# Second feed-forward: the down projection of the last eight tiles by seven products of blocks, with weight sums made by adding DMAs

## The chip, the core and the metric

The kernel runs on one core of a Trainium2 chip. The metric is the device time of one launch in microseconds (us). Executions of this kernel lie close together: three runs gave 1104.26 to 1104.41 us, median 1104.38 us. TensorE (PE) multiplies, VectorE (DVE), ScalarE (ACT) and GpSimd (POOL) work on elements, and SyncE (SP) issues almost all DMAs, in the order of its program.

## What is computed

One layer of a hybrid transformer: a half-step gated feed-forward, a token mixing with attention and a gated MLP, and a second half-step feed-forward. Everything is modulated by vectors made from `c` and `w_ada`. The parts that matter here:

```python
def swiglu(h, w1, w3, w2):
    return (jax.nn.silu(h @ w1) * (h @ w3)) @ w2

def ffn_sublayer(h_in, shift, scale, gate, norm_w, w1, w3, w2):
    h = modulate(rms_norm(h_in, norm_w), shift, scale)
    return h_in + 0.5 * gate * swiglu(h, w1, w3, w2)

mx = jnp.split((jax.nn.silu(c) @ w_ada + b_ada)[:, None, :], N_MOD, axis=-1)
x = ffn_sublayer(x, mx[0], mx[1], mx[2], norm1_w, ffn1_w1, ffn1_w3, ffn1_w2)
...
x = ffn_sublayer(x, mx[6], mx[7], mx[8], norm3_w, ffn2_w1, ffn2_w3, ffn2_w2)
```

`x` has 512 tokens of width 1024, `ctx` 256 tokens; the inner width of a feed-forward is 2816, that is 22 tiles of 128 (`NF`). All values are float32.

## The kernel before

**Three passes for a product.** A float32 operand is split into a rounded part and a remainder ("h" and "l": `st.operand`, `split`, one cast on ACT and one subtraction on DVE), and `mm3` (L173) multiplies h by h, h by l and l by h.

**Start (up to 49 us).** The first scale and shift vectors need 8 MB of `w_ada`, eight steps of two 512 KB rows. For each step k, `first_rows(k)` and `first_raw(k)` load a `scale` tile (1 MB) and a piece of the first up weights (`wfirst`, 256 KB). PE multiplies the rows (L338), ACT and DVE turn the result into one slice of the modulated input (`hfull`, `hh`, `hl`), and PE multiplies that slice with the first weights (L616). Two loads bring the context tokens (`x<-xT 128x8x128`). These loads are pinned to their order among themselves; what has no such pin and waits for nothing is put by the scheduler wherever a queue's model has room. The products of the context tokens follow (L601).

**Up projections by seven products.** From tile 4 on, both feed-forwards compute an up tile f (its two weight blocks by two halves of the width, against two halves of the tokens) in the class `Winograd` by seven block products in place of eight. One unit loads a 1 MB weight block (`st.block`, SP), and POOL makes four sums and differences of its 128x512 quarters in place (`s<-block`, `block<-block`, `block<-s,block`). Each of the seven operands is split by ACT and DVE, up to five ahead of PE (`Flow`, `OPS`; the second feed-forward gets four more, `MORE`). `unit` sends seven products of 12 matmuls through `product`, and small evacuations combine the four banks (`ev_u2z`, `ev_u3`, `ev_lo`, `ev_hi`) into the gated tile `gt[f]`.

**Down projections plainly.** When a chunk of up tiles is ready, `down_thirds` (first feed-forward) or `down_flow` (second) multiplies them with w2, 8 output tiles by n up tiles by 3 passes, and adds to x. The second one's chunks are `CHUNKS2 = [4, 4, 4, 4, 2, 4]`; the last is done by `down` after the loop, with one matmul over 512 columns for each pass and with output DMAs behind each evacuation (L412, L406).

**What sets the order.** The first feed-forward's instructions are placed by the scheduler under dependencies and a pin on parts of the start; in the second the order on PE, DVE, ACT and POOL is that of the program (`nc.ordered`). SP takes its DMAs in the order the scheduler gives, and a DMA that waits for a semaphore holds all DMAs behind it. The wait names DMAHW0 to DMAHW7 are eight semaphores used in turn, so at most eight DMAs of SP are under way.

Of the kernel before, what the change touches and what calls it, by code (L numbers as in the profile page):

```python
# [17 lines left out]
P = 128  # L18
# [12 lines left out]
STEPS_T = (0, 2, 4, 3, 3, 4, 4, 4)  # L31
CHUNKS2 = [4, 4, 4, 4, 2, 4]
NFIRST = 2
# [3 lines left out]
BLOCKS = 2  # L37
# [38 lines left out]
class Halves:  # L76
# [5 lines left out]
    def __getitem__(self, key):  # L82
        i = key[1].start // 512
        return self.tiles[i][:, key[1].start - 512 * i : key[1].stop - 512 * i]


# [95 lines left out]
def layer_kernel(ctx: ExitStack, tc: tile.TileContext, xT, wfirst, wst, wada, wuq, wkpe, cols, wrope, vnw, rope, out):  # L182
# [3 lines left out]

    const = ctx.enter_context(tc.tile_pool(name="const", bufs=1))
    raws = ctx.enter_context(tc.tile_pool(name="raws", bufs=RAWS))
    opp = ctx.enter_context(tc.tile_pool(name="ops", bufs=1))
# [634 lines left out]
    U_UP2 = U_IN + 22  # L824
    U_DN2 = U_UP2 + 44

# [12 lines left out]
    class Winograd:  # L839


        def __init__(self, pool, n, u0, blocks, g_tile, sl_bufs, s1_bufs, third=None, held=None):
            self.third, self.held = third, held
            self.sl_bufs, self.s1_bufs = sl_bufs, s1_bufs
            self.ready = (None,)
            self.pool, self.n, self.u0, self.blocks, self.g_tile = pool, n, u0, blocks, g_tile

        def tmp(self, name, n, bufs=1):
            return self.pool.tile([P, n], F32, tag=name, bufs=bufs, name=f"{name}_{nc.next_id()}")

        def prep(self, f, eng=None, early=False):
            r = st.block(wst, (self.u0 + 2 * f) // 2, self.third if f % 3 == 0 else None)
            q = [r[:, i * 512 : i * 512 + 512] for i in range(4)]
            s1 = self.tmp("s1", 512, self.s1_bufs)
            if f != self.held:
                (eng or nc.gpsimd).tensor_add(s1, q[2], q[3])
            if early:
                eng.tensor_sub(q[2], q[0], q[2])
            self.ready = f, q, s1, nc.gpsimd if early else eng or nc.gpsimd, early

        def wants(self, f):
            q, s1, eng = [], [], []

            def first():
# [6 lines left out]
                return a  # L871

            def block_sums():
                if not self.ready[4]:
                    eng[0].tensor_sub(q[2], q[0], q[2])
                eng[0].tensor_sub(q[0], s1[0], q[0])

# [8 lines left out]
            def third():  # L886
                a = st.operand(q[1])
                eng[0].tensor_sub(q[1], q[1], q[0])
                return a
# [4 lines left out]
        def plan(self, flow, f0, downs, late=False):  # L894
# [3 lines left out]
            flow.todo.append(w[0])  # L898
            for f in range(f0, NF):
                nxt = self.wants(f + 1) if f + 1 < NF else None  # L900
                nx = nxt[:1] if nxt else ()
                if f == self.late:
                    flow.todo.extend((w[3], w[4], w[2]) + nx + (w[1],) + w[5:])
                elif nxt is None:
                    flow.todo.extend((w[3], w[4], w[2], w[1]) + w[5:])
                else:
                    flow.todo.extend(w[1:5] + nx + w[5:])
# [4 lines left out]
        def product(self, bank, blk, first, pend, step=None, cut=False):  # L912
            flow = self.flow
            a = flow.take()
            if blk == "T3" and flow.size > OPS:
                flow.size -= 1
            flow.slot(step or (lambda: None))
            prod(bank, a, self.blocks[blk], self.n, first, cut)
            flow.spent = 1
            flow.pend = [pend] if pend else []  # L920

        def open(self, f, step, f0=None, splits=()):
# [11 lines left out]

            self.product(banks[0], "B11", True, evac(), step)
            return banks, p1

        def unit(self, f, hd, step):
# [7 lines left out]
            def ev_sl():  # L946
                nc.scalar.activation(sl, X, AF.Silu)
                yield

            def ev_u2():  # L950
                v.tensor_add(u2, Y, p1)
                yield

            def ev_u2z():
                v.tensor_add(u2, Y, p1)
                yield
                v.tensor_add(Z, Z, u2)

            def ev_u3():
                nc.scalar.copy(u3, W)  # L960
                v.tensor_add(u3, Z, u3)
                yield

            def ev_lo():
                v.tensor_add(W, W, u2)
                v.tensor_mul(W, W, sl)
# [3 lines left out]
            def ev_hi(seeded=False):  # L970
# [3 lines left out]
                nc.scalar.activation(Z, Z, AF.Silu)  # L974
                v.tensor_mul(Z, Z, u3)
                g_split(Z, gh[:, n:], gl[:, n:])
# [9 lines left out]
            nxt = None  # L986
            if f == self.late or f + 1 == NF:
                self.product(banks[1], "T2", True, ev_u2(), lambda: step(f, 0))
# [5 lines left out]
            else:  # L994
# [3 lines left out]
                self.product(banks[3], "T3", True, ev_u3())  # L998
            seeded = f != self.late and f + 1 < NF
            if f + 1 < NF and nxt is None:  # L1000
                nxt = self.open(f + 1, None)
            self.product(banks[3], "T4", False, ev_lo(), lambda: step(f, 3))
            self.product(banks[2], "B22", False, ev_hi(seeded), cut=n > 256 and f in DOWN1)
            return nxt

        def run(self, flow, f0, after, step=lambda f, i: None, opening=None, splits=()):
# [3 lines left out]
            for f in range(f0, NF):  # L1010
                hd = self.unit(f, hd, step)
                after(self.flow, f)
            flow.slot()
            other_banks()

    def evac_part(pt, dt, g, n):
# [13 lines left out]
    def after1(flow, f):  # L1030
        for ci in ends1(f):
            down_thirds(flow, starts1[ci], CHUNKS1[ci], lambda dt: ada_step(2))

    def ada_up(f, i):
# [3 lines left out]
        elif i < 2:  # L1038
            ada_step()

    t1ctx = ExitStack()
# [1102 lines left out]
    gt.clear()  # L2144
    f2.tile([P, 16], F32, bufs=1, name="pad_f2")

    def g2_tile(f):
        gt[f] = tuple(f2.tile([P, 512], F32R, tag=t, bufs=6, name=f"{t}_{nc.next_id()}") for t in ("gh", "gl"))
        return gt[f]
# [50 lines left out]
    def diffs(i, j, between):  # L2200
# [8 lines left out]
        for k, (hA1, hA2, hB1, hB2) in zip((i, j), q):  # L2209
            s = mod_s[2][0][:, k + 4 : k + 5]  # L2210
            nc.scalar.activation(T2[0][:, k, :], hB2, AF.Identity, bias=s)
            nc.vector.tensor_sub(hA2, hA2, hB2)
        between()
# [10 lines left out]
    def ends2(f):  # L2224
        return [ci for ci in range(len(CHUNKS2) - 1) if starts2[ci] + CHUNKS2[ci] == f]

# [44 lines left out]
    blocks = {"B11": B11, "B21": B21, "B22": B22, "T1": T1, "T2": T2, "T3": T3, "T4": T4}  # L2271
    wino = Winograd(f2, 256, U_UP2, blocks, g2_tile, 2, 2, f2, NPLAIN2 + 1)
    wino.prep(NPLAIN2, nc.vector)
# [23 lines left out]

    def ev3(pt, dt, g, gn):
        evac_lat(pt, dt, 2)
        nc.sync.dma_start(two(out[:, dt, :]), lat(x, dt))  # L2300

    def ev_half(pt, dt, g, gn):
        evac_x(pt, dt, seg_of(g // 256)[:1], 2)
        o = slice(g // 256 * 384, g // 256 * 384 + 256)
        nc.sync.dma_start(out[:, dt, g : g + 256], x[:, dt, o])

    def after2(flow, f):
# [3 lines left out]
    nc.ordered = "all"  # L2311
    st.more = f2ctx.enter_context(tc.tile_pool(name="ops2", bufs=1)), MORE
    wino.run(flow, NPLAIN2, after2, splits=splits)
    nc.ordered = False
    lastu = {}
    last2 = (starts2[-1], CHUNKS2[-1], U_DN2 + starts2[-1])
    down(*last2, [(0, 512)], ev3, range(NK - 1), lastu)
    down(*last2, [(0, 256), (256, 256)], ev_half, range(NK - 1, NK), lastu)
    f2ctx.close()
# [100 lines left out]
```

## Time and profile before

| | |
|---|---|
| median of three runs | 1104.38 us |
| profiled execution, its own time | 1104.5 us |
| span, from the first to the last instruction | 1102.5 us |
| PE busy, share of the span | 1097.5 us, 100% |
| DVE, ACT, POOL busy | 892.8, 536.5, 310.3 us |
| granted clock of PE | 1.00 |
| bytes from HBM, to HBM | 122.58 MB, 2.10 MB |

The difference of 2.0 us between the execution's own time and its span lies outside the instructions. A matmul's busy time is from its start to its modelled end and overlaps the next one's; what PE takes for a stretch of work is read from the chain of waits, which counts from start to start.

### The profile page before, as it was taken

How to read it: one execution, taken by the hardware profiler on the slowest of the kernel's cores; microseconds unless marked ns; L12 is line 12 of the kernel's file. 1: busy time of each engine (PE TensorE's matmuls, PEld its weight loads, DVE VectorE, ACT ScalarE, POOL GpSimd, SP SyncE). 2: the span in 40 equal slices, each digit the busy share in tenths (PEclk: the TensorE clock that was granted, in tenths of full speed). 3: DMA queues.
4: the chain of work that ended last, by engine and by line, in shares of the span. 5: the costliest groups of instructions: out<-in, count | busy, mean ns of one | idle time of the engine just before them, and what ended most of it. 6: DMA issues, size and time to landing. Idle time of an engine off the chain costs nothing.

```text
span 1102.5 us, 19621 instructions
## 1 busy us (share of the span) xinstructions
PE 1097.5 (100%) x7610; PEld 1052.5 (95%) x7610; DVE 892.8 (81%) x1594; ACT 536.5 (49%) x1115; POOL 310.3 (28%) x269
## 2 busy tenths in 40 slices
PE   9999999999999999999999999999999999999998
PEld 7899999999999999999998889999999989898997
DVE  5779998888878769866867899989988878787883
ACT  6545422431344214443765549986663535354450
POOL 0003303311344013400009317860014444352420
PEclk9999999999999999999999999999999999999999
DMA  9721354234334664412241310103222322424202
GB/s 354 279 60 47 120 172 139 100 137 148 106 124 151 233 201 164 149 54 93 97 132 61 102 50 21 39 21 102 91 94 89 123 78 93 137 78 132 99 21 77
DMA packets 35677, 125.95 MB, mean 114 GB/s; under 512 B 3712, under 2 KB 10624, under 8 KB 30976
## 3 DMA queue, kind: packets, MB, share of 16 engines
q1 hardware_dynamic: 35440, 124.63, 33.2%
q8 instruction: 60, 0.98, 0.4%
q14 instruction: 33, 0.27, 0.1%
q10 hardware_dynamic: 144, 0.06, 0.1%
HBM read 122.58 MB, written 2.10 MB: 113 GB/s over the span
## 4 chain that ended last, share of the span: by engine, by line
PE 96%; DMA 1%; DVE 1%; ACT 1%; POOL 0%; issue 0%; SPq 0%; ACTq 0%; POOLq 0%; DVEq 0%
PE mm L60 61%; PE one L60 20%; PE big L60 10%; PE big L616 1%; PE mm L601 1%; DMA scale<-wada 1%; PE mm L177 1%; PE mm L176 1%; PE mm L178 1%; PE mm L338 1%; DMA x<-xT 0%; PE big L608 0%; DVE sq L60 0%; POOL pe L60 0%; ACT hh L60 0%
## 5 line engine op out<-in xcount | busy, mean ns | idle before, releaser
L60 DVE TENSOR_TENSOR opl<-block,oph 128x512 fp32r<-128x512 f32 x216 | 195.4, 912 | 32.6 <-ACT oph L60 29.9
L60 POOL TENSOR_TENSOR block<-block 128x512 f32<-128x512 f32 x69 | 105.0, 1522 | 378.9 <-DVE opl L60 376.2
L60 ACT CAST oph<-block 128x512 fp32r<-128x512 f32 x216 | 132.3, 622 | 108.8 <-PE mm L60 85.5
L60 PE MATMUL mm<-gl,oph 128*128 128x256 f32 (+2 forms) x573 | 176.4, 308 | 0.0
L60 PE MATMUL mm<-gh,opl 128*128 128x256 f32 (+2 forms) x573 | 176.4, 308 | 0.0
L60 PE MATMUL mm<-gh,oph 128*128 128x256 f32 (+2 forms) x573 | 176.4, 308 | 0.0
L60 PEld LDWEIGHTS mm<-gh,oph 128*128 128x128 f32 x573 | 107.6, 188 | 5.5
L60 PEld LDWEIGHTS mm<-gh,opl 128*128 128x128 f32 x573 | 107.6, 188 | 5.4
L60 PEld LDWEIGHTS mm<-gl,oph 128*128 128x128 f32 x573 | 107.6, 188 | 5.4
L60 ACT CAST oph<-raw 128x512 fp32r<-128x512 f32 x127 | 76.0, 620 | 69.7 <-PE mm L60 44.4
L60 DVE SCALAR_TENSOR_TENSOR x<-mm,g,x 128x512 f32<-128x512 f32 (+2 forms) x136 | 78.7, 600 | 28.5 <-PE mm L60 27.9
L60 DVE TENSOR_TENSOR opl<-raw,oph 128x512 fp32r<-128x512 f32 x127 | 88.1, 710 | 15.3 <-ACT oph L60 14.0
L60 POOL TENSOR_TENSOR block<-s,block 128x512 f32<-128x512 f32 x35 | 48.3, 1379 | 123.8 <-DVE opl L60 122.3
L60 PE MATMUL mm<-hh,oph 128*128 128x384 f32 (+2 forms) x195 | 64.9, 333 | 0.0
L60 PE MATMUL mm<-hl,oph 128*128 128x384 f32 (+2 forms) x195 | 64.8, 333 | 0.0
L60 PE MATMUL mm<-hh,opl 128*128 128x384 f32 (+2 forms) x195 | 64.8, 333 | 0.0
L60 DVE SCALAR_TENSOR_TENSOR junk<-raw,cb 128x1024 bf16<-128x1024 f32 x48 | 62.1, 1308 | 0.2 <-DMA raw<-wada 0.2
L60 POOL TENSOR_TENSOR s<-block 128x512 f32<-128x512 f32 x34 | 53.7, 1579 | 11.4 <-DMA block<-wst 11.4
L60 DVE SCALAR_TENSOR_TENSOR raw<-raw,cb 128x1024 f32<-128x1024 f32 x32 | 42.1, 1322 | 8.3 <-DMA raw<-wada 8.2
L60 PE MATMUL one<-hl,oph 128*128 128x384 f32 x144 | 48.1, 334 | 0.0
L60 PE MATMUL one<-hh,oph 128*128 128x384 f32 x144 | 48.1, 334 | 0.0
L60 PE MATMUL one<-hh,opl 128*128 128x384 f32 x144 | 48.1, 334 | 0.0
(699 smaller groups left out, 3361.9 us busy)
## 6 DMA issues: line engine op xcount, KB each, us to landing
raw<-wst SPq DMA_DIRECT2D x77, 512.0 KB, 3.8
block<-wst SPq DMA_DIRECT2D x36, 1024.0 KB, 4.9
raw<-wada SPq DMA_DIRECT2D x56, 512.0 KB, 4.3
scale<-wada SPq DMA_DIRECT2D x16, 512.0 KB, 9.0
x<-xT SPq DMA_DIRECT2D x5, 512.0 KB, 6.4
raw<-wfirst SPq DMA_DIRECT2D x8, 256.0 KB, 8.8
out<-x SPq DMA_DIRECT2D x7, 256.0 KB, 2.3
raw<-wuq SPq DMA_DIRECT2D x2, 384.0 KB, 5.1
```

The costliest lines, as they stand in the source:

```text
L60: return lambda *a, **k: self.tc.keep_in_program_order(f(*a, **k))
L176: nc.tensor.matmul(out, lh, rh, start=first, stop=False, skip_group_check=more)
L177: nc.tensor.matmul(out, lh, rl, start=False, stop=False, skip_group_check=more)
L178: nc.tensor.matmul(out, ll, rh, start=False, stop=last, skip_group_check=more)
L338: pin(nc.tensor.matmul(pa[q, :P], scw[:, kt, 2 - 2 * w : 34 - 2 * w], units[d][w][:, kt * P : kt * P + P], start=w == 0 and kt < 4, stop=w ...
L601: pin(nc.tensor.matmul(o, l[:, c], r, start=k == 0 and m == 0 and w == 0, stop=k == NK - 1 and m == 2, skip_group_check=True))
L616: pin(nc.tensor.matmul(two(pbs[i]), ops[k][lo][:, i * P : i * P + P], lat(r, k), start=False, stop=k == NK - 1 and m == 2, skip_group_chec ...
```

## The change

Of the 22 up tiles of the second feed-forward, the first 14 go down plainly as before, now in chunks 4, 4, 6. The last eight (`SEVEN2 = 14` on) are taken as blocks: 2 halves of the inner width by 2 halves of the output width of w2, against 2 halves of the tokens. Four further units (`unit7`, f = 22 to 25), one for every pair of output tiles j and j + 4, do seven products of 12 matmuls over 256 columns each. The block sums of the gated tiles are made by `Seven.combine` on DVE and ACT while the up units run. Evacuation adds straight into x (`put`), with the gate or its negative.

The weight sums of the up units 14 to 21 and of these four are no longer made by POOL. For each of the 12 a 1 MB buffer in HBM (`block_sums`, shown as `sums_61` to `sums_72`) is filled during the first feed-forward: 48 plain copies of 256 KB, issued by SP, and 48 adding DMAs of 256 KB, issued by POOL. Step by step, `ada_up` and `down_thirds` advance the generator `sum_steps`. The first 24 copies only read weights; the later 24 read a sum that an adding DMA has to have finished. `prep_sums` then loads three quarters of the weight block and the 1 MB of sums. So that the sums are all additions, other operands and evacuations of the second feed-forward change sign.

```diff
-CHUNKS2 = [4, 4, 4, 4, 2, 4]
+CHUNKS2 = [4, 4, 6]
+SEVEN2 = sum(CHUNKS2)
+SUMMED = SEVEN2
...
+    block_sums = [dram.tile([P, 2048], F32, name=f"sums{f}") for f in range(SUMMED, NF + 4)]
...
+        def prep_sums(self, f):
+            a = st.raw_pool.tile([P, 2048], F32, tag="block", bufs=BLOCKS, name=f"block_{nc.next_id()}")
+            src = wst[self.u0 // 2 + f]
+            nc.sync.dma_start(a[:, 0:1024], src[:, 0:1024])
+            pool = self.sums[f % 2]
+            t = pool.tile([P, 2048], F32, tag="block", bufs=1, name=f"s_{nc.next_id()}")
+            nc.sync.dma_start(t, block_sums[f - SUMMED])
+            nc.sync.dma_start(a[:, 1536:2048], src[:, 1536:2048])
...
             def ev_lo():
-                v.tensor_add(W, W, u2)
+                if neg:
+                    v.scalar_tensor_tensor(W, W, -1.0, u2, ALU.mult, ALU.subtract)
...
+                if self.seven and f >= SEVEN2:
+                    self.jobs.extend(self.seven.combine(f, W, Z, gh, gl))
+                    return
...
+        def unit7(self, f, hd):
+            v, j = nc.vector, f - NF
...
+            x_part = (banks[0], blocks["B21"], False, ev_x())
+            self.product(banks[2], blocks["T1"], True, None)
+            last = f + 1 == self.end
+            if not last:
+                self.product(*x_part)
+            self.product(banks[1], blocks["T2"], True, ev_u2z())
+            self.product(banks[3], blocks["T3"], True, ev_w())
+            nxt = self.product(*x_part) if last else self.open(f + 1, None)
+            self.product(banks[3], blocks["T4"], False, ev_lo())
+            self.product(banks[2], blocks["B22"], False, ev_hi())
+            return nxt
...
+        def combine(self, f, W, Z, gh, gl):
...
+            if f % 2 == 0:
+                v.tensor_sub(t1, b12, W)
+                hi(gh, t1)
+                return [lambda: lo(gl, t1, gh)]
...
+            v.tensor_sub(t2, Z, t1)
+            hi(h[0], t2)
+            v.tensor_sub(t3, Z, b12)
...
+        def put(self, pt, dt, g, gate, whole=False):
+            o = x[:, dt, g * 384 : g * 384 + 256]
+            nc.vector.scalar_tensor_tensor(o, pt, gate[:, dt : dt + 1], o, ALU.mult, ALU.add)
+            if whole:
+                self.out(dt, g)
...
+    def sum_steps():
+        q = lambda t, i: t[:, i * 512 : i * 512 + 512]
+        copies, adds = [], []
+        for b in range(0, len(block_sums), 6):
+            for dst, kept, own, more in ((2, None, 0, 2), (0, None, 2, 3), (1, 2, None, 3), (3, 1, None, 1)):
+                for i in range(b, b + 6):
+                    t, w = block_sums[i], wst[U_UP2 // 2 + SUMMED + i]
+                    copies.append((q(t, dst), q(w, own) if kept is None else q(t, kept)))
+                    adds.append((q(t, dst), q(w, more)))
+        nc.sync.dma_start(*copies[0])
+        yield
+        for i, a in enumerate(adds):
+            if i + 1 < len(copies):
+                nc.sync.dma_start(*copies[i + 1])
+            nc.gpsimd.dma_start(*a, accum_op=ALU.add)
+            yield
...
     def ada_up(f, i):
...
+        if i == 0 or i == 3 or i == 1 and f % 4 == 0:
+            next(summing, None)
...
-    nc = bacc.Bacc("TRN2", target_bir_lowering=False, num_devices=1, dynamic_dma_scratch_size=256)
+    nc = bacc.Bacc("TRN2", target_bir_lowering=False, num_devices=1, dynamic_dma_scratch_size=512)
```

The change moves DMAs on the queues, which the diff doesn't tell. The names ending in a number are buffers; `scale` and `raw<-wfirst` are the loads of the start's steps, `x<-xT 128x8x128` the two loads of context tokens, `block<-wst` a unit's weight block.

First place: SP in the start, from the loads of step 2 on. Before, the loads of the eight steps and of the context stand in a row:

```order
L286 DMA raw_148<-wfirst 128x512
L278 DMA scale_150<-wada 128x1024 x2
L286 DMA raw_148<-wfirst 128x512
L278 DMA scale_283<-wada 128x1024 x2
L286 DMA raw_287<-wfirst 128x512
L278 DMA scale_289<-wada 128x1024 x2
L286 DMA raw_287<-wfirst 128x512
L278 DMA scale_293<-wada 128x1024 x2
L286 DMA raw_297<-wfirst 128x512
L268 DMA x<-xT 128x8x128
L278 DMA scale_300<-wada 128x1024 x2
L268 DMA x<-xT 128x8x128
```

Now, on SP at the same place, copies stand among them; these rows go from step 3's last load to step 5's:

```order
L301 DMA raw_163<-wfirst 128x512
L1208 DMA sums_61<-wst 128x512
L1212 DMA sums_62<-wst 128x512
L1212 DMA sums_63<-wst 128x512
L1212 DMA sums_64<-wst 128x512
L1212 DMA sums_65<-wst 128x512
L293 DMA scale_298<-wada 128x1024 x2
L301 DMA raw_302<-wfirst 128x512
L1212 DMA sums_66<-wst 128x512
L1212 DMA sums_61<-wst 128x512
L1212 DMA sums_62<-wst 128x512
L293 DMA scale_304<-wada 128x1024 x2
```

And SP's rows after the next one (another `raw_302`), up to step 7's `scale`; the second context load, `x<-xT 128x8x128`, is the row behind them:

```order
L1212 DMA sums_63<-wst 128x512
L1212 DMA sums_64<-wst 128x512
L1212 DMA sums_65<-wst 128x512
L1212 DMA sums_66<-wst 128x512
L1212 DMA sums_67<-wst 128x512
L293 DMA scale_308<-wada 128x1024 x2
L301 DMA raw_312<-wfirst 128x512
L283 DMA x<-xT 128x8x128
L1212 DMA sums_68<-wst 128x512
L1212 DMA sums_69<-wst 128x512
L1212 DMA sums_70<-wst 128x512
L293 DMA scale_315<-wada 128x1024 x2
```

Five copies now stand ahead of step 4's `scale`, eight ahead of step 5's, 13 ahead of step 6's, and 16 ahead of step 7's and of the second context load; eight more follow among the first weight blocks.

Second place: SP while PE works on the up units 7 to 10 of the first feed-forward, with the semaphores a row waits for (DVE: a buffer set free; DMASW: an adding DMA of POOL done). Before:

```order
L129 DMA block_2515<-wst 128x2048 [waits DVE_49]
L137 DMA raw_2907<-wada 128x1024 [waits DMAHW0_49,DVE_49]
L129 DMA block_2693<-wst 128x2048 [waits DVE_49]
L137 DMA raw_2948<-wst 128x1024 [waits DMAHW1_49,DVE_49]
L129 DMA block_2871<-wst 128x2048 [waits DMAHW3_49,DVE_49]
L137 DMA raw_3001<-wst 128x1024 [waits DMAHW2_49,DVE_49]
```

Now, SP at the same place:

```order
L141 DMA block_2555<-wst 128x2048 [waits DVE_49]
L149 DMA raw_2957<-wada 128x1024 [waits DMAHW6_49,DVE_49]
L1212 DMA sums_61<-sums_61 128x512 [waits DMASW4_49]
L141 DMA block_2739<-wst 128x2048 [waits DVE_49]
L1212 DMA sums_62<-sums_62 128x512 [waits DMASW5_49]
L149 DMA raw_3000<-wst 128x1024 [waits DMAHW7_49,DVE_49]
L1212 DMA sums_63<-sums_63 128x512 [waits DMASW6_49]
L1212 DMA sums_64<-sums_64 128x512 [waits DMAHW0_49,DMASW7_49]
L141 DMA block_2921<-wst 128x2048 [waits DMAHW1_49,DVE_49]
```

The loads of blocks and raws keep their order, but copies that wait for POOL's adding DMAs stand between them.

183 lines of the change are left out of this document (145 added, 38 removed).

## The prediction

> **What bounds the kernel now.** First the page's head: who is busy, and what the chain of waits consists of.
>
> ```profile
> span 1102.5 us, 19621 instructions
> PE 1097.5 (100%) x7610; PEld 1052.5 (95%) x7610; DVE 892.8 (81%) x1594; ACT 536.5 (49%) x1115; POOL 310.3 (28%) x269
> PE 96%; DMA 1%; DVE 1%; ACT 1%; POOL 0%; issue 0%; SPq 0%; ACTq 0%; POOLq 0%; DVEq 0%
> ```
>
> PE is the bound nearly everywhere: a matmul less is time less, and whatever makes PE wait comes on top. The page says "100%" because of its modelled ends, so I look next at the windows, for a place where PE only just keeps up (columns: busy time and count of PE, weight loads, DVE, ACT, POOL, then clock, DMA share, GB/s).
>
> ```profile
> 3.00:30.00 27.00, 26.38 (x272) 21.25 (x271) 16.25 (x30) 16.72 (x36) 0.00 (x0) 1.00 1.05 395
> 30.00:46.00 16.00, 16.00 (x156) 12.52 (x155) 10.17 (x16) 9.28 (x23) 0.00 (x0) 1.00 1.05 377
> 50.00:480.00 430.00, 430.00 (x2914) 429.92 (x2913) 360.30 (x612) 161.68 (x315) 106.10 (x70) 1.00 0.39 133
> 815.00:1100.00 285.00, 284.44 (x2004) 264.62 (x2002) 227.73 (x353) 123.57 (x266) 99.94 (x69) 1.00 0.29 98
> ```
>
> From 3 to 46 us the DMA engines are full (share 1.05, 377 to 395 GB/s) while PE works through the eight start steps. In the first feed-forward (50 to 480 us) and the second (815 us on) they are a third full. So the start stands on two legs, PE and DMA, and the rest on PE alone. The change touches both: it takes matmuls from the end and puts DMAs into the start.
>
> **What the change removes: matmuls.** The chain in the second feed-forward, in order of time (start, length, what):
>
> ```profile
> 869.06 5.44 PE mm L60 x48
> 874.50 1.36 PE one L60 x12
> 875.86 24.53 PE mm L60 x123
> ```
>
> One product of 12 matmuls over 256 columns takes 1.36 us (113 ns each, start to start). The piece of 123 is a down chunk of four tiles, 99 matmuls, with two products of 24 beside it: 24.53 - 2 x 1.36 = 21.81 us for the chunk, 227 ns for 512 columns, so a column costs the same in both shapes. The last eight tiles went down in two such amounts, 43.6 us. Now they take 4 units x 7 products x 1.36 us = 38.1 us. **The saving is 5.5 us**, one eighth. The other tiles do the same columns in other chunks: 0.
>
> **What it adds behind PE in the second feed-forward.** POOL's sums go away for 8 up units. On DVE, `combine` puts 9 operations in a pair of units where two splits stood. I bound that from both sides by rows of DVE near the end, where POOL rests, and by the group of the same splits with POOL at work:
>
> ```profile
> 1069.54 1.89 DVE L142 TENSOR_TENSOR opl<-raw,oph 128x512 fp32r<-128x512 f32 x3
> 1071.35 0.42 DVE L60 TENSOR_TENSOR gl<-mm,gh 128x256 fp32r<-128x256 f32 x1
> 1071.68 0.42 DVE L60 TENSOR_TENSOR mm<-mm,u 128x256 f32<-128x256 f32 x1
> L60 DVE TENSOR_TENSOR opl<-block,oph 128x512 fp32r<-128x512 f32 x93 | 94.2, 1019 | 9.9 <-ACT oph L60 7.9
> ```
>
> A split takes 0.63 us in a row (1.89 / 3), a 256-column operation 0.33 us from start to start. An odd unit has 7 splits, 7 operations as before and 7 of `combine`: 7 x 0.63 + 14 x 0.33 = 9.0 us, against 7 x 1.36 = 9.5 us of PE. An even one has 9 operations: 7.4 us. Both fit, as POOL, under whose work a split averages 1.02 us, is silent there; with 1.02 the odd unit would take 11.8 us and four of them would cost up to 4 x 2.3 = 9 us. I take 0. A `unit7` has 7 splits and about 8 operations, 7.1 us: hidden too. At the hand-over from unit 21, T2 needs its last block only in its tenth matmul, after the products T1 and B21 and nine matmuls: 2 x 1.36 + 1.0 = 3.7 us, for a chain of some six element operations of 0.4 us: hidden, with 1.3 us to spare. Loads per unit grow from 1 MB to 1.75 MB, 184 GB/s over 9.5 us, beside engines that ran at 98: hidden. The tail stays one 256-column evacuation and its output DMA: 0.
>
> **What it adds in the start.** 24 copies are now issued there, because nothing holds them; 16 of them stand ahead of step 7's `scale` and the second context load on SP's queue, and the queue is worked off in its order. Here are the landing times there (issues, size, median from issue to landing) and the rows at which data are used:
>
> ```profile
> scale<-wada SPq DMA_DIRECT2D x16, 512.0 KB, 9.0
> x<-xT SPq DMA_DIRECT2D x5, 512.0 KB, 6.4
> 15.48 0.64 PE L338 MATMUL mm<-scale,sc 128*32 128x128 f32 x16 [0.21 <-DMA scale<-wada]
> 28.40 1.08 PE L338 MATMUL mm<-scale,sc 128*32 128x128 f32 x32
> 40.98 1.08 PE L338 MATMUL mm<-scale,sc 128*32 128x128 f32 x32
> 30.80 0.43 SPq L268 DMA_DIRECT2D x<-xT  x1
> 42.10 0.69 DVE L60 TENSOR_TENSOR sq<-x 128x512 f32<-128x512 f32 x1
> 49.20 11.65 PE mm L601 x95
> ```
>
> PE waited for a `scale` at 15.48 us for the last time; from then on a step comes every 4.2 us ((40.98 - 28.40) / 3), while its 1.25 MB needs 1.31 MB / 395 GB/s = 3.3 us, so DMA gains 0.9 us a step. The second context load is issued at 30.80 and lands 6.4 to 9.0 us later, at 37.2 to 39.8, middle 38.5; it is first needed at 42.10. **The slack is 3.6 us.** Behind it, without a gap to hide in, come squares, a sum by PE, scaling and the split, 7.1 us up to 49.20, where the context products begin. ACT stands in the same queue: its square of that load precedes its copy of step 7's row, so step 7 waits as well.
>
> What one copy costs its queue, c, no row shows: no DMA of before goes from HBM to HBM. Bounds by the nearest rows: at the loads' rate a copy of 262 kB takes 0.262 / 0.395 = 0.66 us. If the saturated 395 GB/s is what passes to and from HBM, a copy counts twice, read and written: 1.33 us. I take 1.33, since the stage's engines have nothing left (1.05) and a copy gives HBM twice the work of a load.
>
> The delay of the start is 16c - 3.6: 16 x 1.33 - 3.6 = **17.7 us**, or 16 x 0.66 - 3.6 = 7.0 us at the other end. Part of it falls on step 4 already (5 copies, 6.7 us less what that step has in hand), but PE's waits don't add up: the last load decides. The other eight copies stand among the first weight blocks, for which PE has the 11.65 us from 49.20 on: 0.
>
> One rule speaks against a cheap copy. The Trainium skill, page "DMA: Bandwidth & Descriptors", section "Latency and other measured facts", gives 207 to 214 GB/s per direction for copies between HBM tensors at full rate. By that, c would be 1.25 us (an estimate from the page), the delay 16.4 us and the time 1115.4 us; no row before shows such a copy, so the next trace decides.
>
> **What it adds in the first feed-forward.** 24 later copies and 48 adding DMAs, of three times 0.262 MB of traffic (read, read, write) each: 24 x 1.33 + 48 x 2.0 = 128 us of full engines in 430 us, beside a share of 0.39: together 0.69. That fits on average. The wait is the danger: SP's copy of a sum waits for an adding DMA that POOL issues only behind its block sums, and the next `block` load is queued behind that copy.
>
> ```profile
> block<-wst SPq DMA_DIRECT2D x36, 1024.0 KB, 4.9
> 201.46 0.33 SPq L129 DMA_DIRECT2D block<-wst  x1
> 197.27 1.30 POOL L60 TENSOR_TENSOR block<-s,block 128x512 f32<-128x512 f32 x1 [1.83 <-DVE opl L60]
> 207.79 1.32 POOL L60 TENSOR_TENSOR s<-block 128x512 f32<-128x512 f32 x1 [0.77 <-DMA block<-wst]
> ACT oph L60 <- PE mm L60: 91.1, 47, 4.9
> 180.95 8.33 PE one L60 x48
> ```
>
> POOL ends that sum at 198.6, issues the add after it, and an add that takes as long as a block's load (4.9 us) is done at 203.5, where the load went out at 201.46: some 2 us late, for which POOL, waiting for it at 207.79 already, has no slack. But ACT waits 91 us in that feed-forward for PE to free operands, so the operands are ready up to five products ahead; a product is 8.33 / 4 = 2.08 us there, five are 10 us. I take 0; the ends are 0 and 8 us, if an add takes twice as long and two units in a row are hit.
>
> **Sum.** The profiled execution took 1104.5 us of its own (span 1102.5; the median of the runs is 1104.38, so the two stand for each other). 1104.5 - 5.5 + 17.7 = 1116.7. I forecast **1116.5 us**.
>
> **Rivals.**
> - **A copy costs no more than a load** (c = 0.66). For: the same queue and engines, the same bytes per DMA; what bounds the 395 GB/s may be the engines, not HBM. Against: full engines leave no room for writes. 1104.5 - 5.5 + 7.0 = 1106.0, not measurably slower. The point from which this decides: c = 9.1 / 16 = 0.57 us is no change at all, and up to 0.70 us the time stays within 0.2%.
> - **Copies hide altogether**, if loads pass them: 1104.5 - 5.5 = 1099.0. Against: one queue, in order.
> - **SP's waits in the first feed-forward starve PE**: 8 us more, 1124.5. For: the loop of block load, sums, add, copy and next load, 4.9 us, three sums of 1.3 us and more, 4.9 us and the waits between, is about as long as a unit, 7 x 2.08 = 14.6 us; against: the 10 us of operands ahead, and long rests of POOL in the down stages.
> - **DVE becomes the bound of the last units**, if splits stay at 1.02 us: up to 9 us more, 1125.5. Against: they were long only beside POOL.
> - **The work isn't moved as said**: PE's columns are in the built order, and the copies too, so no chance worth a number.
>
> **How the numbers follow.** Forecast, 1110 to 1120 with costs of copies between 0.95 and 1.5 us: 0.54. Cheap copies, 1102.3 to 1106.7 for the most part: 0.20. SP's waits: 0.12. DVE: 0.05. Hidden copies, or a gain not seen here: 0.09. A measurement of this kernel tells about 0.2%, 2.2 us, from no change. Faster than that is the last case: 0.09; within it lies most of the cheap copies: 0.18; the rest is slower: 0.73. The range reaches down to the cheap copies and up to the first of the stalls: 1104 to 1123.
>
> **What would show it.** In the profile after: the first context matmul (L601, now 49.20) near 67 us, and waits of PE and ACT for `scale` and `x` between 28 and 60 us, each step right or wrong by them; copies from issue to landing; 5.5 us less between the first up unit of the second feed-forward and the end; opl<-block near 0.69 us in the last units; no waits of PE between 80 and 480 us. Wrong would be: L601 at 55 us (c was a load's), PE gaps in the first feed-forward (SP's waits), or gaps between 1000 us and the end.

## The result and the profile after

The changed kernel takes 1202.93 us in the median (1200.86 to 1203.98), the kernel before 1104.32 us beside it: 1.089 times as long (95% interval 1.087 to 1.091). The forecast of 1116.5 us had the sign and missed the size by 86 us. The profiled execution took 1200.86 us. Two executions below, one of e8 (1552.4 us) and the profiled one of e17 (1351.8 us), ran at granted clocks of 0.66 and 0.75 and are left out of every reading.

The head of its page, and the shares of the chain of waits, can be laid beside the first rows of the prediction:

```profile
span 1199.0 us, 20087 instructions
PE 1127.1 (94%) x7736; PEld 1076.5 (90%) x7736; DVE 895.6 (75%) x1641; ACT 544.0 (45%) x1144; POOL 299.8 (25%) x285
PE 66%; DMA 15%; DVE 7%; issue 7%; POOL 2%; ACT 2%; SPq 0%; ACTq 0%; DVEq 0%; POOLq 0%
```

PE held 96% of the chain before and holds 66% now; DMAs have 15%, waits that the profile gives no releaser for ("issue") 7%. Where that lies is told by three pieces of PE in the chain (start, length, what) that occur in both kernels: the first context products, a piece of 293 matmuls at the end of the first feed-forward, and one of 156 at the beginning of the second. After, then before:

```profile
60.65 11.73 PE mm L616 x96
580.15 51.31 PE mm L62 x293
889.50 17.68 PE mm L62 x156
```

```profile
487.44 51.31 PE mm L60 x293
796.91 17.68 PE mm L60 x156
```

With 49.20 us for the first piece before and the two spans, each stage has a length:

| stage | before | after | difference | forecast |
|---|---|---|---|---|
| start, to the context products | 49.2 | 60.7 | +11.5 | +17.7 |
| first feed-forward, to the piece of 293 | 438.2 | 519.5 | +81.3 | 0 (0 to 8) |
| attention, to the piece of 156 | 309.5 | 309.4 | -0.1 | 0 |
| second feed-forward, to the end | 305.6 | 309.5 | +3.9 | -5.5 |

So 81 of the 96.5 us are the term that I had set to 0. Not all of it is idle time. PE is busy for 460.4 us in this stage, 438.2 before, with 2963 and 2961 matmuls, and its mean granted clock is 0.94 in place of 1.00. So 59.1 us are gaps, and 22.2 us are matmuls that run slower. The page's rows in 40 slices of the span show the clock low where PE has gaps:

```profile
PE   8899959997997966989999999999999999999998
PEclk9899978999998997999999999999999999999999
```

From 182.7 to 187.6 us, for example, behind a gap of 14 us, matmuls over 256 columns follow each other after 213 ns (granted clock 0.54 between 184 and 188 us). From then on they follow after 113 ns at a clock of 1.00.

The waits between 70 and 580 us after (who for whom: total us, times, longest), on POOL, SP's queue and ACT:

```profile
POOL sums L62 <- issue: 90.8, 21, 8.7
POOL s L62 <- DMA block<-wst: 33.4, 10, 7.4
SPq L1212 <- DMA sums<-wst: 180.2, 24, 14.7
ACT oph L62 <- PE mm L62: 69.6, 26, 6.0
ACT oph L62 <- DMA raw<-wst: 62.2, 9, 16.6
```

All 24 later copies (L1212) wait in SP's queue for an add, 180 us in sum. Two pieces of SP's timeline (start, length, line, what) show what stands behind them:

```profile
122.84 16.11 SPq L1212 DMA_DIRECT2D sums<-sums  x3
139.00 0.58 SPq L141 DMA_DIRECT2D block<-wst  x1
139.68 0.38 SPq L149 DMA_DIRECT2D raw<-wst  x1
147.87 10.70 SPq L1212 DMA_DIRECT2D sums<-sums  x2
158.66 1.40 SPq L141 DMA_DIRECT2D block<-wst  x1
```

and POOL's, where the idle time before an instruction stands in brackets:

```profile
147.05 1.30 POOL L62 TENSOR_TENSOR s<-block 128x512 f32<-128x512 f32 x1 [7.42 <-DMA block<-wst]
151.34 0.82 POOL L62 DMA_DIRECT2D sums<-wst  x1
158.39 0.84 POOL L62 DMA_DIRECT2D sums<-wst  x1 [6.22 <-issue]
166.17 0.82 POOL L62 DMA_DIRECT2D sums<-wst  x1 [6.94 <-issue]
```

It is a ring: the copy waits for an add, the block load waits behind the copy, POOL's sum waits for the block (7.42 us), and the next add waits behind that sum. And here an add that directly follows another waits 6 to 7 us for something that the profile doesn't name.

### The profile page after: what moved, and what is told of

Read it like the earlier page. It is cut to its first block, busy times and chain, and to the rows that moved or that the text cites. A ratio compares the mean times of both kernels' runs of the same rounds, so it can differ in the third digit from the quotient of the medians.

```text
span 1199.0 us, 20087 instructions
## 1 busy us (share of the span) xinstructions
PE 1127.1 (94%) x7736; PEld 1076.5 (90%) x7736; DVE 895.6 (75%) x1641; ACT 544.0 (45%) x1144; POOL 299.8 (25%) x285
## 3 DMA queue, kind: packets, MB, share of 16 engines
q0 software_dynamic: 6912, 12.59, 8.1%
## 4 chain that ended last, share of the span: by engine, by line
PE 66%; DMA 15%; DVE 7%; issue 7%; POOL 2%; ACT 2%; SPq 0%; ACTq 0%; DVEq 0%; POOLq 0%
PE mm L62 42%; PE one L62 13%; PE big L62 9%; DMA block<-wst 5%; DMA raw<-wada 3%; DMA sums<-wst 3%; DVE opl L62 2%; DMA scale<-wada 2%; DVE raw L62 2%; DMA raw<-wst 2%; DMA x<-xT 1%; ACT oph L62 1%; POOL block L62 1%; PE mm L616 1%; DVE junk L62 1%
## 5 line engine op out<-in xcount | busy, mean ns | idle before, releaser
L62 DVE TENSOR_TENSOR opl<-block,oph 128x512 fp32r<-128x512 f32 x204 | 176.3, 874 | 65.5 <-ACT oph L62 62.8
L62 ACT CAST oph<-block 128x512 fp32r<-128x512 f32 x204 | 124.5, 621 | 131.1 <-PE mm L62 73.2
L62 POOL TENSOR_TENSOR block<-block 128x512 f32<-128x512 f32 x53 | 84.0, 1586 | 227.1 <-DVE opl L62 225.1
L62 ACT CAST oph<-raw 128x512 fp32r<-128x512 f32 x119 | 70.5, 619 | 102.3 <-DMA raw<-wst 68.2
L62 DVE TENSOR_TENSOR opl<-raw,oph 128x512 fp32r<-128x512 f32 x119 | 82.6, 712 | 40.8 <-ACT oph L62 40.2
L62 DVE SCALAR_TENSOR_TENSOR x<-mm,g,x 128x512 f32<-128x512 f32 (+1 forms) x124 | 68.4, 577 | 35.5 <-PE mm L62 35.4
L62 POOL DMA_DIRECT2D sums<-wst x48 | 39.8, 828 | 113.6 <-issue 90.8
L62 POOL TENSOR_TENSOR block<-s,block 128x512 f32<-128x512 f32 x27 | 37.7, 1397 | 119.6 <-DVE opl L62 118.6
L62 ACT CAST oph<-s 128x512 fp32r<-128x512 f32 x76 | 46.2, 621 | 37.7 <-PE mm L62 22.6
L62 DVE TENSOR_TENSOR opl<-s,oph 128x512 fp32r<-128x512 f32 x76 | 53.4, 703 | 6.8 <-ACT oph L62 5.7
```

The source lines that it names most:

```text
L62: return lambda *a, **k: self.tc.keep_in_program_order(f(*a, **k))
```

## The experiments

Theory Q: loads stand in SP's queue behind copies that were put there too early. Theory R: adds hold POOL, wherever the copies stand. Theory T: the adds' traffic makes the loads late. For the second feed-forward, where 9 us were missing, a theory of its own: the place of its tiles. Stage differences against before, in us, from the same three pieces and the span of each run's profiled execution; times are medians, before lay at 1104.0 to 1104.3 throughout. A profiled execution can lie off its run's median: by 3.5 us below it in e13, 2.7 in e4, 2.1 in the changed kernel, and 2.0 above it in e11; by 1 us or less in the others of this table.

| run | median | start | first ff | attention | second ff |
|---|---|---|---|---|---|
| after | 1202.9 | +11.5 | +81.3 | -0.1 | +3.9 |
| e1_seven | 1117.25 | -0.3 | 0.0 | -0.1 | +13.3 |
| e2_pinned | 1136.2 | -0.2 | +29.7 | -0.3 | +3.3 |
| e3_ring768 | 1171.1 | +9.4 | +54.2 | -0.3 | +3.0 |
| e4_nowait | 1137.9 | +10.5 | +18.2 | -0.6 | +2.8 |
| e5_pin_ring_pad | 1127.9 | -0.3 | +26.8 | -0.4 | -2.4 |
| e6_before_g | 1111.05 | +0.1 | 0.0 | -0.3 | +7.0 |
| e7_seven_pad | 1113.14 | 0.0 | 0.0 | -0.1 | +9.2 |
| e11_noadds | 1102.5 | 0.0 | +3.2 | -0.3 | -2.6 |
| e12_nocopies | 1163.3 | +39.2 | +22.2 | -0.3 | -2.7 |
| e13_plain | 1110.7 | -0.2 | +5.7 | -0.5 | -2.4 |

### The seven products alone

```diff
-SUMMED = SEVEN2
+SUMMED = 99
...
-    summing = sum_steps()
+    summing = iter(())
```

> The seven products alone: no copies and no adding DMAs; POOL makes the sums of all units, the last eight up units and the four down units too. If all of the loss comes from the DMAs of the sums, the start and the first feed-forward are those of before, and the second feed-forward brings the forecast -5.5 us: about 1099 us. If the second feed-forward itself loses (it was 3.9 us longer than before in the changed kernel), about 1108 us or, with POOL's sums for the down units not ready in time, more.

1117.25 us (ratio 1.010 to 1.013). Start and first feed-forward are those of before to 0.3 us: all of their loss comes from the DMAs of the sums. But the second feed-forward is 13.3 us longer, more than with them. DVE's groups in the last 112 us of this run, and in the changed kernel's last 113 us (count | busy us, mean ns):

```profile
L62 DVE TENSOR_TENSOR opl<-block,oph 128x512 fp32r<-128x512 f32 x55 | 51.4, 954 | 0.9 <-ACT oph L62 0.3
```

```profile
L62 DVE TENSOR_TENSOR opl<-block,oph 128x512 fp32r<-128x512 f32 x29 | 19.8, 688 | 2.1 <-ACT oph L62 1.1
```

Beside POOL's sums a split takes 954 ns, without them 688, and DVE, not PE, sets the end: in the chain of e1's last 112 us DVE's splits alone have 34%, PE 16%. The Trainium skill, page "SBUF — State Buffer", section "Who interferes with whom", says that a DVE instruction with two SBUF inputs contends with a GpSimd instruction that reads SBUF; the two rows agree. So the sums by DMA do what they are for in that stage; their price is elsewhere.

### Where the copies stand, and how many adds POOL can have under way

e2 pins the copies to their place in the program and e3 gives POOL's DMAs more descriptor memory. e4 lets the 24 later copies read weights in place of a sum, so that they wait for no add, and pins these 24 as well:

```diff
-        nc.sync.dma_start(*copies[0])
+        pin(nc.sync.dma_start(*copies[0]))
...
-                nc.sync.dma_start(*copies[i + 1])
+                pin(nc.sync.dma_start(*copies[i + 1]))
```

> All copies and adds are kept, but each copy is held at the place where the program writes it, one step ahead of the next add, so that none is drawn forward into the start or ahead of the loads in SP's queue. Theory Q (the loss is loads that stand in SP's queue behind copies issued too early): the start comes back (L601 near 49 us) and most of the 81 us of the first feed-forward, about 1115 to 1130 us. Theory R (the loss is POOL: each adding DMA holds POOL until the add before it has drained, so POOL's own sums come late, wherever the copies stand): only the start comes back, about 1190 us.

```diff
-    const.tile([P, 64], F32, name="pad_scratch")
...
-dynamic_dma_scratch_size=512)
+dynamic_dma_scratch_size=768)
```

> The descriptor memory of POOL's DMAs is 768 bytes in place of 512 (the pad behind it goes, so that all else keeps its address); nothing else changes. Theory R: POOL's idle time ahead of its adds for no shown reason (90.8 us of issue) falls by half or more, and the time by 30 us or more, to 1170 us or less. Theory Q: SP's waits for the adds (180.2 us) stay, 1195 to 1203 us.

```diff
-                    copies.append((q(t, dst), q(w, own) if kept is None else q(t, kept)))
+                    copies.append((q(t, dst), q(w, own or 0)))
...
-                nc.sync.dma_start(*copies[i + 1])
+                (pin if (i + 1) % 24 > 11 else lambda a: a)(nc.sync.dma_start(*copies[i + 1]))
```

> The second and third sums' copies (24 of 48) read the weights in place of an earlier sum, so the sums are not the right ones; the same bytes are moved and the same 48 adds are issued, but no copy waits for an add, and these 24 are held at their place. The first 24 copies stay in the start. Theory Q: SP's 180.2 us of waits for the adds vanish and most of the first feed-forward's 81 us with them, about 1125 to 1140 us, the start's 11.5 us still there. Theory R: POOL's issue stalls stay, over 1170 us.

e2: 1136.2 us; the start is back at 49.05 and 51.6 of the first feed-forward's 81.3 us are gone. e4, with the later copies pinned and without their waits, does as much (1137.9 us); which of the two counts there isn't parted. Q carries the larger part, though e2 stays above the 1130 us that I gave it. But e3, in which SP's order is unchanged, gains 31.8 us too. Its waits, then e2's:

```profile
POOL sums L62 <- issue: 34.1, 11, 7.1
SPq L1212 <- DMA sums<-wst: 147.8, 22, 15.7
```

```profile
POOL sums L62 <- issue: 104.0, 23, 8.9
SPq L1212 <- DMA sums<-wst: 14.9, 1, 14.9
```

With 768 bytes POOL's unnamed waits fall from 90.8 to 34.1 us: that wait is for room for descriptors, and it is one link of the ring. With the copies held it stays (104.0 us), yet SP no longer waits on it. The two theories are two cuts through one ring, and either leaves 18 to 54 us.

### What is left: copies, adds, or the adding

e5 joins e2 and e3 (and moves a pad in the second feed-forward, read below). From it e11 takes the adds, e12 the copies, and in e13 POOL's DMAs copy in place of adding:

> Three things together that act in different stages: the copies held at their place (as in e2_pinned), 768 bytes of descriptors (as in e3_ring768), and the pad in front of the second feed-forward's g tiles put back ahead of them as in the kernel before, so that these start 64 bytes further on while every other operand of TensorE keeps its address. First feed-forward: e2_pinned's +29.7 us shrink by the stalls of POOL that the ring removes, to about +15 (+8 to +22); if traffic is what is left, it stays near +28. Second feed-forward: if the matmuls at 117.7 ns in place of 113.4 come from where the g tiles lie, -4 us against before, near the forecast -5.5; if they come from the change's transfers or from time, +3 as in e2_pinned. Together about 1115 us; 1130 if neither helps.

```diff
-            nc.gpsimd.dma_start(*a, accum_op=ALU.add)
```

> e5_pin_ring_pad without the 48 adds (the sums stay copies of single quarters, so the last units compute something else); the 48 copies stay at their places. First feed-forward, +26.8 us there: if the adds hold it (POOL's own sums behind them, and their traffic), 0 to +5 us; if the copies in SP's queue do, +15 or more.

```diff
+    [pin(nc.sync.dma_start(t, wst[44 + SUMMED + i])) for i, t in enumerate(block_sums)]
...
-        nc.sync.dma_start(*copies[0])
...
-                nc.sync.dma_start(*copies[i + 1])
```

> e5_pin_ring_pad without the 48 copies: twelve copies of whole blocks ahead of the first weights fill the sums once (so they are not the right ones, and the start is some 50 to 100 us later), and the 48 adds stay at their places. Read from L601's product to the piece of 293 matmuls, 438.2 us before and 465.1 in e5_pin_ring_pad: +15 or more if the adds hold the first feed-forward, 0 to +5 if the copies do, and about half each if it is the traffic of both.

```diff
-            nc.gpsimd.dma_start(*a, accum_op=ALU.add)
+            nc.gpsimd.dma_start(*a)
```

> e5_pin_ring_pad with POOL's 48 adding DMAs as plain copies of the same size from the same queue at the same places (the sums are not formed). Without these DMAs the first feed-forward lost 3.2 us, with them and without the other copies 22.2, with both 26.8. If it is the adding (a read of the destination more, and slower packets) that takes the loads' time, 5 to 12 us of loss; if it is that POOL issues and waits, and any DMA of its queue does the same, 20 us or more.

In e5 the larger memory gave only 2.9 us more than e2: my +15 was wrong. POOL's unnamed waits fell to 14.4 us, but it now waits for the copies instead (54.0 us for `sums<-sums`). Of the 26.8 us left, the copies alone make 3.2, the adds alone 22.2, and plain DMAs in the adds' place with the copies 5.7. By these profiled executions the adding itself costs 21 us; by the medians of e5 and e13 it is 17. The queues' rows between 60 and 487 us (packets, MB, share of 16 engines' time), of before, e5 and e13:

```profile
q1 hardware_dynamic: 13536, 56.47, 38.9%
```

```profile
q1 hardware_dynamic: 19261, 66.75, 46.1%
q0 software_dynamic: 6624, 12.06, 22.7%
```

```profile
q0 software_dynamic: 3840, 12.59, 13.0%
```

48 adds have 6912 packets on the page, 144 each, so 6624 are 46. They take 0.227 x 427 / 46 = 2.1 us of all sixteen engines each, a plain copy from the same queue 0.130 x 427 / 48 = 1.16 us. The loads' median landings in the kernel before, in e12 and in e11 (issues, size, us):

```profile
block<-wst SPq DMA_DIRECT2D x36, 1024.0 KB, 4.9
raw<-wada SPq DMA_DIRECT2D x56, 512.0 KB, 4.3
```

```profile
block<-wst SPq DMA_DIRECT2D x28, 1024.0 KB, 7.1
raw<-wada SPq DMA_DIRECT2D x56, 512.0 KB, 5.3
```

```profile
block<-wst SPq DMA_DIRECT2D x28, 1024.0 KB, 4.9
raw<-wada SPq DMA_DIRECT2D x56, 512.0 KB, 4.7
```

Beside adds without copies (e12) a block takes 7.1 us, beside copies without adds (e11) 4.9 as before. That fits theory T: longer landings in a stage that reuses each buffer at once. But e13 speaks against it as the whole account. The blocks' median landings between 60 and 487 us, of e5 and then of e13:

```profile
block<-wst SPq DMA_DIRECT2D x16, 1024.0 KB, 7.9
```

```profile
block<-wst SPq DMA_DIRECT2D x16, 1024.0 KB, 7.6
```

Beside plain DMAs the blocks land almost as late, and the stage loses 5.7 us in place of 26.8. What e13 does not have are POOL's unnamed waits, 14.4 us in e5 and 40.3 in e12. So the 17 to 21 us are the price of the adding, but whether it is paid in landings or in POOL's delay behind its own DMAs stays open.

### The second feed-forward: 64 bytes

In the changed kernel the g tiles (the moving operand of the down pieces) start 64 bytes earlier than before, because a pad went behind them. PE's pace, in the chain of the changed kernel from the first down piece on:

```profile
908.54 25.12 PE mm L62 x123
933.66 5.65 PE one L62 x48
...
970.40 25.21 PE mm L62 x123
995.61 5.44 PE one L62 x48
```

The prediction's rows show the same pieces before. A piece of 123 takes 25.12 us in place of 24.53, four products 5.65 in place of 5.44, until the next down piece ends; then 5.44 again, and 5.65 once more behind the third down piece. Nothing waits, and the granted clock is 1.00. e6 moves the pad in the kernel before, e5 and e7 move it back in e2/e3 and e1:

```diff
-    f2.tile([P, 16], F32, bufs=1, name="pad_f2")
...
+        f == 0 and f2.tile([P, 16], F32, bufs=1, name="pad_f2")
```

> The kernel before with one change: the 64 byte pad of the second feed-forward stands behind its g tiles in place of ahead of them, so that the g tiles start 64 bytes earlier, as in the changed kernel; no other operand moves. If where the g tiles lie sets TensorE's pace, long stretches of the second feed-forward run at 117.7 ns per 256-column matmul and the time is 5 to 9 us more, 1109 to 1113 us. If not, 1104.4 us.

> e1_seven (no copies, no adds, POOL's sums to the end) with the g tiles 64 bytes further on, as in the kernel before. Its slow stretches cost about 4.5 us by the spacing of the matmuls, so about 1112.7 us if they come from the place of the g tiles; the rest of its loss, the last 115 us in which VectorE is busy 95% of the time, stays. 1117 us if the place is not the cause.

e6 turns slow at the same piece and recovers at the same piece as the changed kernel:

```profile
815.74 25.12 PE mm L60 x123
840.86 5.65 PE one L60 x48
...
877.61 25.21 PE mm L60 x123
902.82 5.44 PE one L60 x48
```

1111.05 us, 7.0 us more than before for 64 bytes (ratio 1.005 to 1.008). e7 gains 4.1 us over e1, and e5's second feed-forward is 2.4 us shorter than before's: against e2, where the g tiles lay as in the changed kernel, place accounts for 3.3 + 2.4 = 5.7 us. With the g tiles moved back the stage is 9.2 us longer than before with POOL's sums (e7) and 2.4 us shorter with sums by DMA (e5): that is what these are worth, 11.6 us.

### Sums made elsewhere

From here on the steps stand behind the first feed-forward's units, on the larger memory and with the g tiles moved back. e8 gives one step to each load of the attention. e9 makes only the sums from unit 20 on, and e10 shifts the seven products' tiles by 64 bytes. e14 makes all of them again, leads the copies by three steps and shifts these tiles by 320 bytes. e15 leaves the tiles where e8 had them and gives no step to the attention's score products; e16 is e15 with the tiles shifted by 256 bytes. e17 and e18 also leave the last down piece free and start at unit 16 and 18. The first edits are e8's, the last one e18's:

```diff
-            down_thirds(flow, starts1[ci], CHUNKS1[ci], lambda dt: (ada_step(2), dt % 2 and next(summing, None)))
+            down_thirds(flow, starts1[ci], CHUNKS1[ci], lambda dt: ada_step(2))
...
-        if i == 0 or i == 3 or i == 1 and f % 4 == 0:
-            next(summing, None)
...
+    st.step = lambda: next(summing, None)
...
-SUMMED = SEVEN2
+SUMMED = 18
```

> As e5_pin_ring_pad, but the copies and adds are issued behind the first feed-forward's units: one step at each load of the attention, from the last down piece of the first feed-forward on, and two steps per load near the end. The start and the first feed-forward are then those of before (L601's product near 49 us, the piece of 293 matmuls near 487 us). If the attention's loads and POOL's work there leave room, its 309 us stay and the second feed-forward's -4 us remain: about 1100 us, faster than both. If POOL's 35 us of attention work or the loads come late behind the adds, 1108 us or more.

> As e8_att, but only the last two up units and the four down units take sums made by DMAs (24 copies and 24 adds in place of 48 and 48); POOL makes the sums up to unit 19. In the kernels without DMA sums the second feed-forward falls only 1.9 us behind up to unit 18, and 10 us after it. The steps stand at the first feed-forward's last down piece and at the loads behind the attention, away from POOL's own attention work. Attention: 7.4 us of loss shrink to 0 to 2; second feed-forward: -2.5 plus 0.5 to 2 for the units left to POOL. 1102 to 1106 us; 1108 or more if the burst at the down piece is what held the attention in e8_att.

> As e9_att20, with the tiles of the seven products (the last eight tiles' blocks and their sums) 64 bytes further on. Their last 45 us run 2 to 4% slow in every kernel so far. If this is the place again, 1 to 1.5 us less than e9_att20; if not, the same.

> e8_att (all 48 copies and 48 adds behind the first feed-forward's units) thinned out: one step per load, the rest one per unit of the second feed-forward, each copy three steps ahead of its add in place of one, so that POOL does not wait for it; and the seven products' tiles 320 bytes further on, at the same place within 512 bytes as the g tiles. Attention: e8_att's +7.4 us fall to 0 to 3, if POOL's waits of 60 us for copies made them; second feed-forward -2.5 to -4. 1101 to 1105 us; above 1106 if the adds' traffic or the issue itself holds the attention.

> e14_lead448 with no step during the attention's 32 products with the weighted scores, in which POOL works 80% of the time and PE lost 2.4 of the attention's 3.0 us; those steps go to the loads behind it, two per load, and to the first units of the second feed-forward. The seven products' tiles lie as in the changed kernel. If POOL's adds held the scores: attention +0.5 to +1, second feed-forward -2 to -2.5, about 1102.5 to 1103.5 us, a little below the kernel before. If the adds take from the attention wherever they stand, +3 again and 1105.5 or more.

> As e15_quiet, with the seven products' tiles 256 bytes further on, so that they lie within 512 bytes as the operands of the up units do, which run at 113.4 ns there. If place alone sets the pace of the last 45 us (1.02 to 1.03 of the up units' time in the changed kernel's place, 1.05 at the two others tried), about 1 us less than e15_quiet; the same or more if it is the mixture of tiles of several places.

> e15_quiet without the steps at the first feed-forward's last down piece (there 480 to 530 us lost 2.1 us) and with DMA sums only from unit 16 on (40 copies and 40 adds, in one group of ten blocks). If the crowding of adds at a place is what costs: attention 0 to +1, second feed-forward -1 to -2, 1102 to 1104 us, at or a little below the kernel before. If every add costs wherever it stands, 1106 us again.

> As e17_from16 with DMA sums only from unit 18 on (32 copies and 32 adds). Fewer adds, and two more units on POOL's sums, which cost about 1 us up to unit 18 in e7_seven_pad: the same as e17_from16 within 1 us if crowding is the cost, 1102 to 1104 us; 1 us less than it if every add costs.

| run | median | ratio to before, interval | to the piece of 156 | second ff |
|---|---|---|---|---|
| e8_att | 1108.6 | 1.003 to 1.006 | +7.4 | -2.4 |
| e9_att20 | 1105.64 | 1.000 to 1.002 | -0.4 | +2.0 |
| e10_att20_s7 | 1106.80 | 1.001 to 1.003 | +1.5 | +1.5 |
| e14_lead448 | 1108.82 | 1.003 to 1.006 | +2.8 | -0.7 |
| e15_quiet | 1106.75 | 1.002 to 1.003 | +3.8 | -1.1 |
| e16_quiet384 | 1106.11 | 1.000 to 1.002 | +2.4 | -0.8 |
| e17_from16 | 1106.4 | 1.002 to 1.004 | no reading | no reading |
| e18_from18 | 1103.05 | 0.998 to 1.000 | +0.2 | +0.5 |

The stages are again those of the profiled executions; e18's was the slowest of its run, 1.9 us above the median, and e14's the fastest, 2.1 below. Most expectations here were too good, e8's by 9 us and the others by 2 to 5; e9, e16 and e18 came out about as expected. e8's loss lies in the attention: POOL's score products come late beside the adds (PE waits 2.2 us for `pe` directly), and loads at the last down piece. Each placement gave one loss back and kept or opened another, e15's at the last down piece, e9's in the units left to POOL. e14 to e16 are also some 1.5 us slower in the second feed-forward than e8; its first units carry the remaining steps there, but I did not part that from the tiles' places. Crowding is not the whole cost: e17, without the crowded place, is no better than e15. e18, with 32 adds in place of 48, is 1.1 us below before, an interval that ends at 1.000: not a gain that this measurement can call one. Of the places of the seven products' tiles, those shifted by 64 and 320 bytes (e10, e14) ran the last 45 us at about 1.047 of the up units' time per matmul, the unshifted one (e8) and the one shifted by 256 (e16) at 1.02 to 1.03: place matters there too, and none tried was clean.

## Why the prediction was wrong, step by step

- **The failed step is the first feed-forward: "I take 0; the ends are 0 and 8 us". It was +81.3.** The DMA time was right: I counted 128 us of full engines, and the changed kernel's stage shows 0.59 x 519.5 - 0.39 x 438.2 = 136 us more than before. What doesn't follow from "That fits on average" is that each load lands in time. The rival "SP's waits" had the place, the loop and its rows, and was priced at two late units, 8 us; the wait comes with all 24 copies. Three of its numbers were off: an add lands after 6.3 us in the median, not 4.9; adds in a row wait for room on POOL, which no row of before could show; and the loads behind them take 6.9 us, not 4.9. By the runs: held copies give back 51.6, what is left is 26.8 with the larger memory, of which the adding has 17 to 21. And no term of mine had the matmuls behind a gap: 22.2 of the 81.3 us are PE's longer busy time at a granted clock of 0.94, and 8.6 of e5's 26.8.
- **I compared the wait with ACT's 91 us of rest**, a sum of 47 waits. The rest is at most 10 us in one place, as I wrote; SP's holds are 10.7 and 16.1 us long, one unit after the other.
- **The start: +11.5, forecast 17.7, bounds 7.0 and 17.7.** The mechanism holds: with the copies held it is 49.05 us. The size of c was off: (11.5 + 3.6) / 16 = 0.94 us by my formula, not 1.33. In e12 12 x 1.05 MB ahead of the weights cost 39.2 us, 0.82 us per 0.262 MB, or 321 GB/s each way. The Trainium skill's 207 to 214 GB/s ("DMA: Bandwidth & Descriptors", "Latency and other measured facts") would make 1.25 us (an estimate from the page). The page gives them for tensors whose rows lie 512 KB or more apart, here they lie 8 KB apart; the rate is too low for these copies, and the measurement decides.
- **The saving: -5.5 forecast, +3.9 found.** With the g tiles where they were it is -2.4 to -2.7 (e5, e11, e12). The rest, about 3 us, stands in the last 45 us, which run 2 to 3% slow, and in 1.5 to 2 us of waits there; I had set the hand-over and `unit7` to 0.
- **DVE: right.** Splits take 688 ns in the last units, as "near 0.69" asked; with POOL at work (e7) the stage is 11.6 us longer than with sums by DMA, where the rival said up to 9, for four of these units.
- **What I did not weigh:** the moved pad. I took tiles that lie 64 bytes elsewhere for the same tiles.

## What to carry to other kernels

A share of busy engines says whether transfers fit in a stage, not whether they land in time: where buffers are used up at once, ask what a longer landing and a wait at the head of the one load queue do to the next load; count the slower matmuls behind a gap too, 22 of 81 us here; and pin transfers that no one is waiting for to the place where they are wanted. Before transfers take over work from an engine, price them where they are made: here 48 adds cost 22 us in a stage with 39% of its DMA time taken and 2 to 7 us behind it, for 11.6 us of gain. And when tiles move by a few bytes, compare the spacing of the matmuls before looking for waits.

## What was unexpected in the hardware

- 64 bytes of difference in where a moving operand starts change TensorE's pace by 2.8% over 512 columns (before 226.8 ns from start to start in the first down piece, 233.3 in e6) and by 3.8% over 256 columns (5.44 to 5.65 us for 48), at a granted clock of 1.00; the slower pace then holds through up units whose own operands haven't moved, until a down piece ends. Why it persists stays open.
- An adding DMA of 256 KB between buffers in HBM took 2.1 us of all sixteen engines (e5), a plain copy of the same queue 1.16 (e13); its landing was 6.3 to 6.8 us, the plain copy's 4.9.
- With 512 bytes of descriptor memory POOL waited at 21 of 48 adding DMAs, up to 8.7 us and 90.8 us in sum; with 768 bytes (e3) at 11, 34.1 us in sum.
- Behind a gap of 14 us matmuls over 256 columns stood 213 ns apart for 5 us, in place of 113 ns, at a granted clock near one half (0.54).
